# Tiny per-head products moved from VectorE to GpSimd in a two-layer decoder trunk

## The chip, the cores and the metric

One core of one Trainium2 chip runs the whole kernel in one launch. The metric is the device time of that launch in microseconds (us); smaller is better. The engines are named as in the profile: PE is TensorE's matrix multiply, PEld its weight load, DVE is VectorE, ACT is ScalarE, POOL is GpSimd and SP is SyncE, which here issues the loads. Each engine has a queue of its own and works through it in order; a wait at the head of a queue holds everything behind it.

## The reference

The input is x of 256 tokens by 2048 features and a memory of 256 tokens. There are two layers. Layer 0 projects x, sends 1536 columns through a causal pooling mixer and the last 512 through a cross-attention over the memory with 4 heads of 128, projects the joined result, and then runs a squared-ReLU MLP of width 8192. Shared keys and values are then made once. Layer 1 projects x into queries of 12 differential heads (two maps of 64 per head) and 4 memory heads:

```python
def rms_norm(x, g):
    xf = x.astype(jnp.float32)
    y = xf * lax.rsqrt(jnp.mean(xf * xf, axis=-1, keepdims=True) + EPS)
    return (y * g.astype(jnp.float32)).astype(x.dtype)
...
        a = probs(q1b, k1) - lam * probs(q2b, k2)
        return jnp.einsum('bhqk,bkhd->bqhd', a.astype(v.dtype), v)
...
            o = differential_attention(q1, q2, sk1, sk2, sv, lam)
            token_out = (rms_norm(o, subln_norm[b]) * (1.0 - lam_init)).reshape(B, S, DIFF_V_WIDTH)
...
        mem_out = memory_cross_attention(mem_q, mem, mem_norm[i], w_mem_kv[i], mem_q_norm[i], mem_k_norm[i])
        x = x + jnp.concatenate([token_out, mem_out], axis=-1) @ w_out[i]
        x = x + squared_relu_mlp(rms_norm(x, ffn_norm[i]), w_ff1[i], w_ff2[i])
```

EPS is 1e-6. All arithmetic is float32 in the reference.

## The kernel before

**Weights.** All weights lie in memory in the order of use and stream through a ring. For each quad of four 128x128 blocks, ACT makes the rounded high half (`hi_ring`, L157) and DVE the remainder (`lo_ring`, L158: one subtraction of two SBUF tiles). PE multiplies with both halves. The ring has 6 slots, and a quad is prepared up to 3 quads ahead of its use (`Feed.fill`). A quad keeps PE busy for about 1.4 us.

**Attention beside the weights.** The work of the heads is put between the quads. `at(d, fn)` files a function for d quads later, and `tick()` runs what is due after each quad. A differential head (`diff_head`) has four steps. `scores` multiplies queries and keys into PSUM, adds the mask on DVE, takes the row maximum on DVE (`mx`, L1207), multiplies it by the query's scale (L1208), runs four exponentials on ACT (L1211, with their row sums in `z`), and forms `att` from them with reciprocals on DVE. Four quads later `turn` transposes the result on PE (`dt`, L1226). `pv` multiplies by the values and does the per-head RMS norm: two squares with sums on ACT (`o_ss`), `o_v` on DVE, then `rsqrt_cols`, then two scalings into `osb` (L1250). `back` transposes `osb` (`o_t`, L1255) and splits it into `cat`. The third group of four heads lies under the memory queries' projection and is packed closer (`by_pe`: PE adds the mask).

`rsqrt_cols` takes a column of 2 to 16 values per row through ln and exp on ACT (L359, L360), then makes one step of refinement with two products on DVE (L361, L362) and one combined operation (L300).

A memory head has `mem_query` (squares, `stats` two quads later with `rsqrt_cols`) and `mem_head` (scores, maximum `mm_max` at L575 and L576, exponentials, a transposition `mt` at L592, and the product with the values). `mem_head` serves both layers; `mem_query` serves layer 1 alone.

**The order on each queue.** The order in which the program calls instructions is not the order on the engines. A scheduler of the framework places each engine's instructions by when it reckons them ready, and puts semaphore waits between engines.

**Stages in the trace.** Layer 0's heads lie at 84 to 125 us. Layer 1's differential heads and memory heads run from about 1150 to 1276 us, under the projections `q` and `mq` and the start of the output projection `wo`. After that come the residual, the MLP of layer 1, and the end.

Of the kernel before, what the change touches and what calls it, by code (L numbers as in the profile page):

```python
# [13 lines left out]
AF = mybir.ActivationFunctionType  # L14
ALU = mybir.AluOpType
# [3 lines left out]
P = 128  # L19
# [3 lines left out]
EPS = 1e-6  # L23
LAM_INIT = 0.8 - 0.6 * math.exp(-0.3)
# [8 lines left out]
G_PS, G_MQ, G_MK, G_QN, G_KN, G_SUB = 112, 124, 126, 128, 129, 130  # L33
# [229 lines left out]
def program(ctx, tc, plan, dry, xT, memT, par, lam, cst, wst, yT):  # L263
    nc = tc.nc
# [28 lines left out]
    def vt(name):  # L293
        return tp.tile([P, T], F32, tag="v", bufs=6, name=name)
# [4 lines left out]
    def stt(out, a, s, b, op0, op1, **kw):  # L299
        nc.vector.scalar_tensor_tensor(out=out, in0=a, scalar=s, in1=b, op0=op0, op1=op1, **kw)  # L300
# [39 lines left out]
    def gcol(c):  # L340
        return param[:, c : c + 1]
# [10 lines left out]
        stt(t2, mean, EPS, t, ALU.add, ALU.mult)  # L352
        stt(out, t2, 3.0 * CN * CN, h, ALU.subtract, ALU.mult, reverse0=True)

    def rsqrt_cols(out, v):

        n = v.shape[-1]
        w = [tp.tile([P, 16], F32, tag="w8", bufs=8, name="rc")[:, :n] for _ in range(4)]
        nc.scalar.activation(w[0], v, AF.Ln)  # L359
        nc.scalar.activation(w[1], w[0], AF.Exp, bias=lnc, scale=-0.5)  # L360
        nc.vector.tensor_mul(w[2], w[1], w[1])  # L361
        nc.vector.tensor_mul(w[3], w[2], v)  # L362
        stt(out, w[3], 3.0 * CN * CN, w[1], ALU.subtract, ALU.mult, reverse0=True)

    def stat(name):
        return pp.tile([P, T], F32, tag="st", bufs=1, name=name)
# [174 lines left out]
    def mem_query(src, gq, cols):  # L541


        q = vt("mq")
        sq = vt("mq_sq")
        nc.scalar.activation(q, src, AF.Copy, scale=gq)
        nc.scalar.activation(sq, src, AF.Square)
        y = tp.tile([P, 2], F32, tag="m2", bufs=12, name="mq_y")

        def stats():  # L550
            st = stat("st_mq")
            for t in range(2):
                nc.tensor.matmul(
                    st[:, 2 * t : 2 * t + 2], sq[:, t * P : t * P + P], ones_h,
                    start=True, stop=True,
                )
            v2 = tp.tile([P, 2], F32, tag="m2", bufs=12, name="mq_v")
            nc.vector.tensor_mul(v2, st[:, 0:4].rearrange("p (a b) -> p a b", b=2)[:, :, 0], cols[1])
            nc.vector.tensor_scalar_add(v2, v2, EPS)
            rsqrt_cols(y, v2)  # L560
            nc.vector.tensor_mul(y, y, cols[0])

        at(2, stats)
        return q, y

    def mem_head(q, y, k, v, e, pT, out, lag, pv_lag=6):

        def scores():  # L570
            s = pp.tile([P, 2, T], F32, tag="s", bufs=2, name="ms")
            for t in range(2):
                nc.tensor.matmul(s[:, t, :], q[:, t * P : t * P + P], k, start=True, stop=True)
            m = tp.tile([P, 2], F32, tag="m2", bufs=12, name="mm_max")
            nc.vector.tensor_reduce(out=m, in_=s, axis=AX.X, op=ALU.max, negate=True)  # L575
            nc.vector.tensor_mul(m, m, y)  # L576
            z = tp.tile([P, 2], F32, tag="m2", bufs=12, name="mm_sum")
            for t in range(2):
                nc.scalar.activation(
                    e[:, t, :], s[:, t, :], AF.Exp, bias=m[:, t : t + 1], scale=y[:, t : t + 1],  # L580
                    accum_out=z[:, t : t + 1],
                )
            zr = tp.tile([P, 2], F32, tag="m2", bufs=12, name="mm_rec")
            nc.vector.reciprocal(zr, z)
            for t in range(2):
                nc.vector.tensor_scalar_mul(e[:, t, :], e[:, t, :], zr[:, t : t + 1])

        def turn():
            t4 = pp.tile([P, 2, T], F32, tag="t", bufs=1, name="mt")
            for mb in range(2):  # L590
                for t in range(2):
                    nc.tensor.transpose(  # L592
                        t4[:, mb, t * P : t * P + P], e[:, t, mb * P : mb * P + P], ident
                    )
            nc.scalar.copy(pT, t4)

        def pv():
            o = pp.tile([P, T], F32, tag="o", bufs=1, name="mo")
            for mb in range(2):
                nc.tensor.matmul(o, v(mb), pT[:, mb, :], start=mb == 0, stop=mb == 1)  # L600
            nc.scalar.copy(out[:, 0:T], o)
            nc.vector.tensor_sub(out[:, T : 2 * T], o, out[:, 0:T].bitcast(F32))

        at(lag, scores)
        at(lag + 4, turn)
        at(lag + pv_lag, pv)
# [557 lines left out]


    gsub = cp.tile([P, 1], F32, name="gsub")
    nc.vector.tensor_scalar_mul(gsub, gcol(G_SUB), 1.0 - LAM_INIT)
    idb = cp.tile([P, P], BF16, name="idb")
    nc.vector.tensor_copy(idb, ident)
    mkb = cp.tile([P, P], BF16, name="mkb")  # L1170
# [4 lines left out]
    def diff_head(h, q, y, lag, pv_lag, back_lag, by_pe):  # L1175
# [3 lines left out]
        yh = y.rearrange("p (t j m h) -> p t j m h", t=2, j=2, m=2)[:, :, j % 2, :, h % 2]  # L1179
        ez = tp.tile([P, 2], F32, tag="ez", bufs=6, name="ez")  # L1180

        def scores():
            s1 = pp.tile([P, 2, T], F32, tag="s", bufs=2, name="s1")
            s0 = pp.tile([P, 2, P], F32, tag="s", bufs=2, name="s0")
            if by_pe:
                for m in range(2):
                    kk = kT[:, 6 * m + j, :]
                    nc.tensor.matmul(s1[:, m, :], q[:, m, P:T], kk, start=True, stop=False)
                    nc.tensor.matmul(s1[:, m, P:T], idb, mkb, start=False, stop=True)
                for m in range(2):  # L1190
                    kk = kT[:, 6 * m + j, 0:P]
                    nc.tensor.matmul(s0[:, m, :], q[:, m, 0:P], kk, start=True, stop=False)
                    nc.tensor.matmul(s0[:, m, :], idb, mkb, start=False, stop=True)
            else:
                for m in range(2):
                    kk = kT[:, 6 * m + j, :]
                    nc.tensor.matmul(s1[:, m, :], q[:, m, P:T], kk, start=True, stop=True)
                for m in range(2):
                    kk = kT[:, 6 * m + j, 0:P]
                    nc.tensor.matmul(s0[:, m, :], q[:, m, 0:P], kk, start=True, stop=True)  # L1200
                mask = const[:, C_MASK : C_MASK + P].unsqueeze(1).to_broadcast([P, 2, P])
                nc.vector.tensor_add(s1[:, :, P:T], s1[:, :, P:T], mask)
                nc.vector.tensor_add(s0, s0, mask)
            mx = tp.tile([P, 2, 2], F32, tag="m4", bufs=6, name="mx")
            z = tp.tile([P, 2, 2], F32, tag="m4", bufs=6, name="z")
            for t, s in ((1, s1), (0, s0)):
                nc.vector.tensor_reduce(out=mx[:, t, :], in_=s, axis=AX.X, op=ALU.max, negate=True)  # L1207
            nc.vector.tensor_mul(mx, mx, yh)  # L1208
            for t, s, e in ((1, s1, e1), (0, s0, e0)):
                for m in range(2):  # L1210
                    nc.scalar.activation(  # L1211
                        e[:, m, :], s[:, m, :], AF.Exp, bias=mx[:, t, m : m + 1],
                        scale=yh[:, t, m : m + 1], accum_out=z[:, t, m : m + 1],
                    )

            zr = tp.tile([P, 2], F32, tag="m2", bufs=12, name="zr")
            nc.vector.reciprocal(zr, z[:, :, 1])
            stt(zr, zr, nlam, z[:, :, 0], ALU.mult, ALU.mult)
            stt(ez, z[:, :, 0], EPS, z[:, :, 0], ALU.mult, ALU.mult)
            for t, e, dst in ((1, e1, a[:, P : P + T]), (0, e0, a[:, 0:P])):  # L1220
                stt(dst, e[:, 1, :], zr[:, t : t + 1], e[:, 0, :], ALU.mult, ALU.add)

# [6 lines left out]
        def pv():  # L1229
            o = pp.tile([P, 2, P], F32, tag="o", bufs=1, name="do")  # L1230
# [5 lines left out]
            if by_pe:  # L1236
                nc.vector.tensor_copy(osb, o)
                o = osb
            ss = tp.tile([P, 2], F32, tag="m2", bufs=12, name="o_ss")
            junk = vt("o_sq")  # L1240
            for t in range(2):
                nc.scalar.activation(
                    junk[:, t * P : t * P + P], o[:, t, :], AF.Square, accum_out=ss[:, t : t + 1]
                )
            v = tp.tile([P, 2], F32, tag="m2", bufs=12, name="o_v")
            stt(v, ss, 1.0 / P, ez, ALU.mult, ALU.add)
            yo = tp.tile([P, 2], F32, tag="m2", bufs=12, name="o_y")
            rsqrt_cols(yo, v)
            for t in range(2):
                nc.vector.tensor_scalar_mul(osb[:, t, :], o[:, t, :], yo[:, t : t + 1])  # L1250

# [12 lines left out]
    for c in range(3):  # L1264
        ps = pair_of_banks(0, "q1")
        b_tile(ps, "w_in_q", 1, c, x_mx)
        rows, v = query_rows(ps, c1, 64)
        rope(rows, qtab)
        y = query_scale(v, c1)
# [10 lines left out]
    for h in range(4):  # L1280
        ps = mmt("mq1")
        c_tile(ps, "w_in", 1, 12 + h, range(NK), x_mx)
        q, y = mem_query(ps[:, 0:T], mqg1, c1)
# [93 lines left out]
```

## Time and profile before

| | |
|---|---|
| median of 3 runs | 2045.62 us (2045.5 to 2046.13) |
| the profiled execution's own time | 2044.93 us |
| its span, first to last instruction | 2043.1 us |
| PE busy | 2037.2 us |
| DVE busy | 1716.2 us, 3215 instructions |
| ACT busy | 1349.8 us, 2505 instructions |
| POOL busy | 51.9 us, 67 instructions |
| granted TensorE clock | 1.000 of full speed |

The span is the time between the first and the last instruction on the core; the execution's own time is 1.83 us longer. Busy times are sums of the durations of an engine's instructions, without their overlaps. Instructions of one engine can overlap in these records by up to a tenth of a microsecond or so, since the next one starts while the last results of the one before are being written.

### The profile page before, as it was taken

How to read it: one execution, taken by the hardware profiler on the slowest of the kernel's cores; microseconds unless marked ns; L12 is line 12 of the kernel's file. 1: busy time of each engine (PE TensorE's matmuls, PEld its weight loads, DVE VectorE, ACT ScalarE, POOL GpSimd, SP SyncE). 2: the span in 40 equal slices, each digit the busy share in tenths (PEclk: the TensorE clock that was granted, in tenths of full speed). 3: DMA queues.
4: the chain of work that ended last, by engine and by line, in shares of the span. 5: the costliest groups of instructions: out<-in, count | busy, mean ns of one | idle time of the engine just before them, and what ended most of it. 6: DMA issues, size and time to landing. Idle time of an engine off the chain costs nothing.

```text
span 2043.1 us, 32257 instructions
## 1 busy us (share of the span) xinstructions
PE 2037.2 (100%) x11060; PEld 1755.3 (86%) x11060; DVE 1716.2 (84%) x3215; ACT 1349.8 (66%) x2505; POOL 51.9 (3%) x67
## 2 busy tenths in 40 slices
PE   9999999999999999999999999999999999999999
PEld 8888888888888888888888888888888888888888
DVE  8888889889879978999766687889879978988997
ACT  7765566666666756768665697566657666666764
POOL 0001200000000000000000000310000000000000
PEclk9999999999999999999999999999999999999999
DMA  9556556555555555655565543656555555565564
GB/s 314 178 181 190 188 174 206 197 196 197 186 201 202 189 207 191 207 169 182 194 228 186 170 140 103 196 166 207 196 196 205 186 196 196 186 210 195 196 209 135
DMA packets 110470, 390.75 MB, mean 191 GB/s; under 512 B 12256, under 2 KB 14944, under 8 KB 110304
## 3 DMA queue, kind: packets, MB, share of 16 engines
q1 hardware_dynamic: 110160, 388.59, 57.1%
q8 instruction: 86, 1.41, 0.3%
q14 instruction: 80, 0.66, 0.1%
q10 hardware_dynamic: 144, 0.10, 0.0%
HBM read 386.54 MB, written 2.10 MB: 190 GB/s over the span
## 4 chain that ended last, share of the span: by engine, by line
PE 99%; ACT 1%; DVE 1%; issue 0%
PE x_bank L391 33%; PE x_bank L393 16%; PE wo L391 6%; PE p L746 5%; PE p L747 5%; PE p L748 5%; PE wo L393 3%; PE u L391 2%; PE ff L391 2%; PE u L393 1%; PE k L417 1%; PE k L419 1%; PE v L417 1%; PE k L418 1%; PE v L419 1%; PE v L418 1%
## 5 line engine op out<-in xcount | busy, mean ns | idle before, releaser
L157 ACT CAST hi_ring<-raw 128x512 fp32r<-128x512 f32 x1193 | 736.7, 620 | 529.5 <-PE x_bank L391 308.0
L158 DVE TENSOR_TENSOR lo_ring<-raw,hi_ring 128x512 fp32r<-128x512 f32 x1193 | 817.2, 695 | 206.7 <-ACT hi_ring L157 165.5
L391 PE MATMUL x_bank<-fx,hi_ring 128*128 128x512 f32 x1920 | 602.1, 395 | 0.0
L393 PEld LDWEIGHTS x_bank<-fx,lo_ring 128*128 128x128 f32 x1920 | 361.0, 188 | 83.6
L393 PE MATMUL x_bank<-fx,lo_ring 128*128 128x256 f32 x1920 | 377.4, 278 | 0.0
L391 PEld LDWEIGHTS x_bank<-fx,hi_ring 128*128 128x128 f32 x1920 | 301.4, 189 | 9.3
L391 PE MATMUL x_bank<-z,hi_ring 128*128 128x512 f32 x960 | 301.1, 395 | 0.0
L158 DVE TENSOR_TENSOR lo_ring<-slab,hi_ring 128x1024 fp32r<-128x1024 f32 x188 | 230.1, 1224 | 54.3 <-ACT hi_ring L157 53.6
L157 ACT CAST hi_ring<-slab 128x1024 fp32r<-128x1024 f32 x188 | 196.9, 1047 | 73.1 <-PE x_bank L391 36.2
L393 PEld LDWEIGHTS x_bank<-z,lo_ring 128*128 128x128 f32 x960 | 180.5, 188 | 41.7
L393 PE MATMUL x_bank<-z,lo_ring 128*128 128x256 f32 x960 | 188.8, 278 | 0.0
L391 PE MATMUL wo<-cat,hi_ring 128*128 128x512 f32 x512 | 162.5, 398 | 0.5 <-DVE resid L639 0.5
L391 PEld LDWEIGHTS x_bank<-z,hi_ring 128*128 128x128 f32 x960 | 151.9, 189 | 6.5 <-ACT room L672 0.4
L393 PEld LDWEIGHTS wo<-cat,lo_ring 128*128 128x128 f32 x512 | 95.9, 188 | 21.7
L672 ACT COPY room<-x_bank 128x512 f32<-128x512 f32 x180 | 104.9, 583 | 2.0 <-PE x_bank L393 2.0
L393 PE MATMUL wo<-cat,lo_ring 128*128 128x256 f32 x512 | 101.4, 279 | 0.0
L746 PE MATMUL p<-hi_ring,sit 128*128 128x512 f32 x256 | 100.5, 393 | 0.0
L747 PE MATMUL p<-hi_ring,sit 128*128 128x512 f32 x256 | 100.2, 391 | 0.0
L748 PE MATMUL p<-lo_ring,sit 128*128 128x512 f32 x256 | 99.7, 389 | 0.0
L391 PEld LDWEIGHTS wo<-cat,hi_ring 128*128 128x128 f32 x512 | 79.1, 189 | 2.2 <-PE wo L393 0.9
L717 ACT ACTIVATE room<-room 128x256 f32<-128x256 f32 x128 | 53.2, 416 | 39.1 <-DVE room L300 39.1
L746 PE MATMUL p<-hi_ring,z 128*128 128x512 f32 x192 | 75.2, 392 | 0.0
(313 smaller groups left out, 3102.3 us busy)
## 6 DMA issues: line engine op xcount, KB each, us to landing
raw<-in_w SPq DMA_DIRECT2D x595, 512.0 KB, 4.0
slab<-in_w SPq DMA_DIRECT2D x124, 512.0 KB, 3.3
resid<-in_x SPq DMA_DIRECT2D x8, 256.0 KB, 5.9
room<-in_w SPq DMA_DIRECT2D x4, 512.0 KB, 4.2
memraw<-in_mem SPq DMA_DIRECT2D x4, 512.0 KB, 3.6
out_y<-resid SPq DMA_DIRECT2D x16, 128.0 KB, 1.8
memraw<-in_mem SPq DMA_DIRECT2D x7, 256.0 KB, 6.3
raw<-in_w SPq DMA_DIRECT2D x3, 256.0 KB, 3.5
```

What stands on the lines that cost most here:

```text
L157: self.nc.scalar.copy(hi, src)
L158: self.nc.vector.tensor_sub(lo, src, hi.bitcast(F32))
L391: nc.tensor.matmul(ps, hi, xs[:, k, :], start=first and c == 0, stop=False)
L393: nc.tensor.matmul(ps[:, T : 2 * T], lo, xs[:, k, 0:T], start=False, stop=last and c == len(ks) - 1,)
L417: nc.tensor.matmul(ps[t], xl, hi, start=k == 0, stop=False)
L418: nc.tensor.matmul(ps[t], xh, hi, start=False, stop=False)
L419: nc.tensor.matmul(ps[t], xh, lo, start=False, stop=k == NK - 1)
L672: nc.scalar.copy(x, ps)
L717: at(3, lambda: nc.scalar.activation(stage[i % 8], y[:, 0:T], AF.Square))
L746: nc.tensor.matmul(ps, a[1], hi, start=first, stop=False)
L747: nc.tensor.matmul(ps, a[0], hi, start=False, stop=False)
L748: nc.tensor.matmul(ps, a[0], lo, start=False, stop=last)
```

## The change

It concerns operations on two or four columns (128 rows by 2 or 4 values). In `rsqrt_cols`, when called for a differential head's norm or a memory query of layer 1, the two products go to GpSimd. So do the product of the memory query's scale with the row's factor, the products of the maxima with the scales in `mem_head` (both layers) and `diff_head`, the square `ez`, and the sum `o_v`. [...]

```diff
-    def rsqrt_cols(out, v):
+    def rsqrt_cols(out, v, aside=False):
...
+        eng = nc.gpsimd if aside else nc.vector
...
-        nc.vector.tensor_mul(w[2], w[1], w[1])
-        nc.vector.tensor_mul(w[3], w[2], v)
+        eng.tensor_mul(w[2], w[1], w[1])
+        eng.tensor_mul(w[3], w[2], v)
...
-            rsqrt_cols(y, v2)
-            nc.vector.tensor_mul(y, y, cols[0])
+            rsqrt_cols(y, v2, True)
+            nc.gpsimd.tensor_mul(y, y, cols[0])
...
-            nc.vector.tensor_mul(m, m, y)
+            nc.gpsimd.tensor_mul(m, m, y)
...
-    nc.vector.tensor_scalar_mul(gsub, gcol(G_SUB), 1.0 - LAM_INIT)
+    nc.vector.tensor_scalar_mul(gsub, gcol(G_SUB), (1.0 - LAM_INIT) * EPS**-0.5)
...
-            nc.vector.tensor_mul(mx, mx, yh)
+            nc.gpsimd.tensor_mul(mx, mx, yh)
...
-            stt(ez, z[:, :, 0], EPS, z[:, :, 0], ALU.mult, ALU.mult)
+            nc.gpsimd.tensor_mul(ez, z[:, :, 0], z[:, :, 0])
...
                 nc.scalar.activation(
-                    junk[:, t * P : t * P + P], o[:, t, :], AF.Square, accum_out=ss[:, t : t + 1]
+                    junk[:, t * P : t * P + P], o[:, t, :], AF.Square,
+                    scale=(P * EPS) ** -0.5, accum_out=ss[:, t : t + 1],
                 )
...
-            stt(v, ss, 1.0 / P, ez, ALU.mult, ALU.add)
+            nc.gpsimd.tensor_add(v, ss, ez)
...
-            rsqrt_cols(yo, v)
+            rsqrt_cols(yo, v, True)
```

The scheduler places the instructions of the changed kernel anew. In the built order PE's queue differs first where the differential heads' transpositions start, and last early in `wo`; the rest of it is the same instruction for instruction.

## The prediction

> **What bounds the kernel now.** I read the page's busy line first, then the stretches around layer 1's heads, then DVE's groups by shape there, then timelines of single heads.
>
> ```profile
> PE 2037.2 (100%) x11060; PEld 1755.3 (86%) x11060; DVE 1716.2 (84%) x3215; ACT 1349.8 (66%) x2505; POOL 51.9 (3%) x67
> ...
> 1150.00:1170.00 20.00, 19.91 (x104) 16.62 (x103) 14.06 (x38) 14.68 (x39) 0.00 (x0) 1.00 0.43 143
> 1170.00:1190.00 20.00, 19.78 (x106) 16.61 (x105) 18.21 (x67) 17.99 (x53) 0.00 (x0) 1.00 0.37 127
> 1190.00:1210.00 20.00, 20.00 (x121) 17.78 (x120) 16.76 (x56) 16.15 (x53) 0.00 (x0) 1.00 0.52 159
> 1210.00:1230.00 20.00, 19.95 (x156) 18.76 (x155) 18.08 (x64) 17.84 (x55) 0.00 (x0) 1.00 0.42 132
> 1250.00:1270.00 20.00, 19.24 (x116) 16.66 (x116) 16.79 (x60) 14.90 (x52) 0.00 (x0) 1.00 0.31 106
> 1270.00:1290.00 20.00, 19.68 (x113) 16.76 (x112) 17.26 (x33) 11.55 (x25) 5.59 (x7) 1.00 0.56 181
> ```
>
> PE bounds it. A row of the second kind is a stretch of 20 us with the busy time of PE, PEld, DVE, ACT and POOL. DVE reaches 18 of 20 us under the heads, yet PE is idle for only 0.09 + 0.22 + 0.05 + 0.76 + 0.32 = 1.44 us there, and its granted clock is 1.00. Two short restarts after waits add perhaps 1 us that counts as busy. So what a lighter DVE can win is at most about 2.4 us: PE's own work is not changed.
>
> ```profile
> L361 DVE TENSOR_TENSOR rc<-rc 128x2 f32<-128x2 f32 x16 | 2.5, 157 | 1.3 <-ACT rc L360 1.3
> L300 DVE SCALAR_TENSOR_TENSOR ez<-z 128x2 f32<-128x2 f32 x12 | 1.9, 160 | 6.8 <-ACT att L1211 6.7
> L1208 DVE TENSOR_TENSOR mx<-mx,qy 128x4 f32<-128x4 f32 x12 | 1.9, 159 | 0.1
> ```
>
> **What leaves DVE.** Each differential head loses `mx`, `ez`, `o_v` and two `rc`: 12 x 5 = 60. Each memory head of layer 1 loses two `rc` and two products: 16. Layer 0's heads lose one each: 4. That is 80 instructions of about 0.157 us, 12.5 us of DVE's busy time. Less of it is queue time: in a timeline the next independent instruction starts 0.07 to 0.11 us after such a product (1170.44 to 1170.50), so about 7 us. And `ez` stands in a wait anyway (6.7 us idle before it, for ACT), after which the reciprocal waits for ACT again.
>
> **What an operation on POOL costs.** The trace has none on two columns with two inputs. The nearest rows are a memset of 128x2 at 0.10 us and a product of 128x256 at 0.61 us; scaled by columns between them it is about 0.1 us. I take 0.12, since two columns lie next to the memset, and keep 0.10 and 0.61 as ends. From DVE's end to POOL's start the trace has 0.08 to 0.18 us (L639 to L624 and L618), from POOL to POOL 0.09. From POOL to ACT there is no row; DVE to ACT takes 0.04 (1156.97 to 1157.00), and 0.04 to 0.2 is taken. So `mx` costs 0.13 + 0.12 + 0.05 = 0.30 us from the last maximum to the first exponential, where it cost 0.23 (1156.77 to 1157.00): +0.07 per head.
>
> The Trainium skill says in "GPSIMD Engine Reference", section "Engine selection", that elementwise work with two inputs is about twice as slow there; taken as an estimate that makes 0.31 us of 0.157, still under the upper end above.
>
> **The lock.** POOL and DVE do disturb each other:
>
> ```profile
> 200.28 0.61 POOL L624 TENSOR_TENSOR psq<-resid 128x256 f32<-128x256 f32 x1 [3.75 <-DVE resid L639]
> 200.98 1.07 POOL L625 TENSOR_TENSOR acc<-acc,psq 128x256 f32<-128x256 f32 x1
> ...
> 200.59 0.86 DVE L158 TENSOR_TENSOR lo_ring<-raw,hi_ring 128x512 fp32r<-128x512 f32 x1 [0.38 <-ACT hi_ring L157]
> ```
>
> The sum started at 200.98, inside the `lo_ring` subtraction that ended at 201.45, and ended at 202.05: 0.60 us after DVE was done, as long as POOL's product takes alone. It was held until DVE finished. At 183.50 the same: DVE ended at 183.70, POOL at 184.30. The Trainium skill states this in "SBUF — State Buffer", section "Who interferes with whom": a DVE instruction with two SBUF inputs and a GpSimd one that reads SBUF exclude each other, and the later one waits out the whole instruction. The trace agrees (0.60 us above).
>
> Here that means that a product on POOL which comes just after a `lo_ring` (0.69 us) has started costs up to 0.6 us more, and one that comes ahead of it delays DVE by 0.12 at most.
>
> **Who waits.** Head 1 and head 3 show the two places:
>
> ```profile
> 1155.76 1.01 DVE L1207 TENSOR_REDUCE mx<-s 128x2 f32<-128x512 f32 x2
> 1156.81 0.16 DVE L1208 TENSOR_TENSOR mx<-mx,qy 128x4 f32<-128x4 f32 x1
> 1157.24 0.69 DVE L158 TENSOR_TENSOR lo_ring<-raw,hi_ring 128x512 fp32r<-128x512 f32 x1 [0.27 <-issue]
> ...
> 1160.47 0.52 PE L1226 MATMUL dt<-const,att 128*128 128x128 f32 x3
> ```
>
> In the built order a `lo_ring` follows the maxima directly in heads 1, 2, 3 and 5 of the first eight. In head 2 it waits for ACT's cast until after POOL would be done (1164.19 against 1163.95), and in head 5 ACT is busy with other work meanwhile. So two are held in full: 1 and 3. ACT waits at its first exponential, with the next casts behind it; the casts feed slots which PE reads 4 to 10 us later (from the end of each subtraction to PE's first use), so that is covered. If that cover is gone, a late cast stops PE directly. At the turns of the three groups it is thinner: 1.37 us (1183.74), 0.75 (1215.63) and 0.71 (1283.52).
>
> What is not covered is `dt`. From the end of `att` to `dt` the twelve heads have 0.14, 0.87, 0.15, 1.46, 0.92, 0.72, 0.42, 1.50, 4.23, 0.15, 1.00 and 0.56 us, of which about 0.1 is the signal. A delay of 0.07 is lost in these. Heads 1 and 3 with 0.6 lose 0.46 + 0.45 = 0.9 us of PE.
>
> The norm's chain: `o_y` on DVE now waits for ACT's Exp and two products on POOL. In head 3 Exp ends at 1169.89; POOL 0.08 + 0.12 + 0.09 + 0.12 and 0.1 for the signal make 1170.40, where before the second product was through at 1170.59. DVE's next item before `o_y` ends at 1170.08, so DVE stands idle for about 0.3 us, with a mask addition, two scalings and two maxima behind it. That takes back what the five removed instructions gave (5 x 0.08 = 0.4). `o_t` comes 1.3 to 6 us after `osb`, except head 6, where PE waits (1217.04) and the new order has `osb` ahead of a `lo_ring`: 0.2 us won.
>
> Memory heads of layer 1: `mt` follows the scaled `att` by 0.90 and 0.10 us and then waits twice (0.76 us is the longest PE stall here). Its chain now changes engine five times, at +0.1 us each, but skips DVE's queue, which took 3.1 us from Exp (1256.99) to the exponentials (1260.10). I put this at zero, with 1 us either way. Layer 0's four `mx` have 2.2 us (`mt` at 90.69, `att` at 88.51): nothing. The scaled square and `gsub` cost nothing: same instructions with other constants.
>
> **Sum.** Lost 0.9; won 0.4 (0.2 at head 6's `o_t`, 0.2 of the 0.68 us that PE idles outside the memory heads' stall); memory heads 0: +0.5 us. On the profiled execution 2044.93 becomes 2045.4; the median stands 0.69 above it, so 2045.62 becomes about 2046.1. That is no change: 0.2%, 4.1 us, is about what a measurement of this kernel can tell from none.
>
> **Rivals.**
> - *The lock holds nearly every product* (slower). If each head's chain comes late by 0.6 us, the `dt` slacks give 0.46 + 0.45 + 0.18 + 0.45 + 0.04 = 1.6 us and the memory heads (0.90, 0.10, none, none) 1.7: 2048.9. At 1.0 us late they give 4.1 and 3.0: 2052.7. It decides from 0.7 us per head (2.1 + 2.0). For it: the hold of a full `lo_ring` is 0.69 us, and there are up to four products in a chain. Against it: DVE has such subtractions for about half of the time, and cat, mask and maximum read PSUM. This is the rule named above, taken at its worst.
> - *DVE's relief wins* (faster). All 1.44 us of idle PE and the restarts go: 2043.2 to 2044.2, which is still within 0.2%. Faster than that needs a gain that no row shows.
> - *The reordering decides.* ACT puts four exponentials (2.0 us) ahead of a cast in the third group, and PE's queue is shuffled until `wo`. With 0.7 to 1.4 us of cover at three turns, 1 us late costs 0.3 each, 2 us late up to 1.3 each: 2046.5 to 2049.5, mostly within 0.2%.
>
> **Chances.** Forecast 0.50, relief within 0.2% 0.13, reordering within 0.2% 0.12: together 0.75 the same. Lock and reordering beyond 4.1 us: 0.21 slower. Faster by more: 0.04. The likeliest gives 2046.1. The range goes from 2043.5 (nearly all idle PE won) to 2051.0 (chains late by 0.9 us), leaving out some 0.15.
>
> **What would show it.** POOL has 80 more instructions, mostly 0.1 to 0.2 us, some near 0.7 beside a `lo_ring`. DVE's busy time falls by some 12 us, and new DVE waits for POOL stand at `o_y`, 0.2 to 0.4 us each. PE's idle time between 1145 and 1290 us stays within 1 to 3 us. The forecast is wrong if products on POOL take over 0.6 us on their own, if PE waits for `lo_ring`, or if `dt` and `mt` wait in most heads.

## The result

The kernel with the change takes 2048.7 us (median of 22 runs, 2048.26 to 2050.12), the kernel before it 2045.32 us on the same chip (22 runs, 2045.0 to 2046.48). The ratio of the two is 1.0017, with a 95% interval of 1.0011 to 1.0023. So the change costs 3.4 us. That is inside the 0.2% that was set as "no change", and inside the predicted range. But it is a loss that the interval tells from nothing, and it is 2.6 us above the forecast of 2046.1 us.

The profiled execution of the changed kernel took 2048.7 us with a span of 2046.9 us, 3.8 us more than before. Some 0.5 us of these are there at 50 us already, long before anything that the change touches, and still at 1150 us: that is the start-up's own spread (one of the runs below, e5_split, has 1.6 there). The rest arises between 1150 and 1290 us.

The first line is the page's busy line, the others the same stretches of 20 us that the prediction showed (PE, PEld, DVE, ACT, POOL, granted clock, DMA share, GB/s), now of the changed kernel.

```profile
PE 2039.0 (100%) x11060; PEld 1753.9 (86%) x11060; DVE 1708.0 (83%) x3135; ACT 1349.3 (66%) x2505; POOL 73.6 (4%) x147
...
1150.00:1170.00 20.00, 19.92 (x102) 16.43 (x101) 13.51 (x33) 14.57 (x37) 0.91 (x5) 1.00 0.46 148
1170.00:1190.00 20.00, 19.27 (x106) 16.20 (x105) 17.06 (x52) 17.23 (x53) 2.43 (x11) 1.00 0.41 129
1190.00:1210.00 20.00, 19.75 (x111) 17.15 (x110) 14.63 (x41) 15.63 (x51) 3.31 (x14) 1.00 0.42 141
1210.00:1230.00 20.00, 19.67 (x150) 18.06 (x150) 16.17 (x51) 18.66 (x58) 2.62 (x11) 1.00 0.39 127
1230.00:1250.00 20.00, 19.25 (x148) 17.63 (x146) 13.90 (x41) 15.41 (x54) 4.66 (x18) 1.00 0.32 106
1250.00:1270.00 20.00, 18.97 (x121) 16.20 (x121) 14.54 (x44) 15.23 (x52) 5.26 (x18) 1.00 0.26 80
1270.00:1290.00 20.00, 20.00 (x115) 17.13 (x114) 15.99 (x30) 11.83 (x24) 4.96 (x6) 1.00 0.52 177
```

Eighty instructions left DVE and POOL has eighty more, as built. DVE is lighter in every one of these stretches, and PE is idle in six of the seven, for 0.08 + 0.73 + 0.25 + 0.33 + 0.75 + 1.03 = 3.17 us in place of 1.44. The granted clock stays at 1.00. One of these stretches of the kernel before the prediction does not show; PE was never idle in it:

```profile
1230.00:1250.00 20.00, 20.00 (x157) 18.80 (x157) 15.34 (x56) 16.20 (x56) 0.00 (x0) 1.00 0.25 80
```

The growth of the idle time, 1.7 us, is only about half of the loss. PE's busy time grew too, by 1.8 us for the same 11060 matmuls (2037.2 to 2039.0). The prediction had put such time down to restarts after waits; the runs do not say where it lies.

The new groups on POOL, by shape (us busy in total, mean ns of one, then the idle time before them):

```profile
L1249 POOL TENSOR_TENSOR o_v<-o_ss,ez 128x2 f32<-128x2 f32 x12 | 3.9, 322 | 33.4 <-ACT o_sq L1244 33.4
L1210 POOL TENSOR_TENSOR mx<-mx,qy 128x4 f32<-128x4 f32 x12 | 3.7, 306 | 919.1 <-DVE mx L1209 914.1 <-DVE rc L364 5.0
L1221 POOL TENSOR_TENSOR ez<-z 128x2 f32<-128x2 f32 x12 | 2.3, 195 | 19.6 <-ACT att L1213 19.6
L578 POOL TENSOR_TENSOR mm_max<-mm_max,qy 128x2 f32<-128x2 f32 x4 | 2.2, 544 | 107.7 <-DVE mm_max L577 107.7
L578 POOL TENSOR_TENSOR mm_max<-mm_max,mq_y 128x2 f32<-128x2 f32 x4 | 1.7, 430 | 1.9 <-DVE mm_max L577 1.9
```

A product of two or four columns takes 0.20 us on POOL (`ez`, at 195 ns), where DVE took 0.16. The groups with a larger mean contain single instructions of 0.34 to 1.05 us. There are 14 of these among the 80, and they sum to 8.5 us. With the other 66, at about 0.20, they make 21.5 us, and POOL's busy time has grown by 21.7.

Head 3 shows one of the 14. First POOL, then DVE, then PE, from the timelines:

```profile
1173.24 0.58 POOL L1210 TENSOR_TENSOR mx<-mx,qy 128x4 f32<-128x4 f32 x1 [2.05 <-DVE mx L1209]
1172.16 1.01 DVE L1209 TENSOR_REDUCE mx<-s 128x2 f32<-128x512 f32 x2
1173.09 0.68 DVE L158 TENSOR_TENSOR lo_ring<-raw,hi_ring 128x512 fp32r<-128x512 f32 x1
1177.32 0.52 PE L1228 MATMUL dt<-const,att 128*128 128x128 f32 x3 [0.47 <-DVE att L300]
```

The maxima end at 1173.17. Before POOL has its signal, DVE starts the next `lo_ring` subtraction, which ends at 1173.77, and the product on POOL ends at 1173.82, 0.05 us later. Twelve of the 14 are in layer 1, and all twelve end 0.05 to 0.10 us after a DVE subtraction of two SBUF tiles: eleven after a `lo_ring`, one after `room`. Three and a half microseconds on, PE waits 0.47 us at `dt`.

The norm's chain of head 1, which stands on DVE just ahead of head 3's maxima, POOL and then DVE:

```profile
1170.72 0.20 POOL L363 TENSOR_TENSOR rc<-rc 128x2 f32<-128x2 f32 x1 [0.64 <-ACT rc L362]
1171.00 0.20 POOL L364 TENSOR_TENSOR rc<-rc,o_v 128x2 f32<-128x2 f32 x1
1171.23 0.16 DVE L300 SCALAR_TENSOR_TENSOR o_y<-rc 128x2 f32<-128x2 f32 x1 [0.48 <-POOL rc L364]
```

DVE stands idle for 0.48 us, with a mask addition, two scalings and the two maxima behind `o_y`. That is how head 3's maxima come to end next to a ready `lo_ring`: counted from the first `tq` they end 1.0 us later than before (22.95 us against 21.93), and 0.9 us later already with the norm's part alone (e3_norm below). The step behind them did not get longer. From the last maximum to the first exponential head 3 took 1.06 us before, when the product stood behind other work in DVE's queue, and 0.69 with the change, its hold included.

Two answers of the view of waits, first of DVE and ACT, then of PE, between 1145 and 1310 us (what waited, for what; us in total, times, longest):

```profile
DVE o_y L300 <- POOL rc L364: 7.7, 11, 1.3
ACT att L1213 <- POOL mx L1210: 3.7, 7, 1.1
```

```profile
PE dt L1228 <- DVE att L300: 0.7, 2, 0.5
PE o_t L1258 <- DVE mq_v L560: 0.6, 1, 0.6
PE ms L575 <- ACT att L1213: 0.5, 1, 0.5
PE dt L1228 <- ACT att L1165: 0.2, 1, 0.2
...
```

Three more waits of 0.2 us follow, at `tq`, `s` and `do`. None of these stands in the same view of the kernel before, and the two that did (0.76 us at `mt` and 0.33 at `wo`) are gone.

The second of the two waits at `dt` (0.25 us, 1203.38, head 6) has no held `mx` behind it: that head's product took 0.20 us, but its maxima ended 2.0 us later than before, counted from the first `tq`. Ahead of them DVE waited 0.86 us at an `o_y` (1197.66) whose `o_v` had taken 0.64 us, held by a `lo_ring` (1195.88).

### The profile page after: what moved, and what is told of

Same layout as the page of the kernel before. It is cut to its first block, busy times and chain, and to the rows that moved or that the text cites. A ratio compares the mean times of both kernels' runs of the same rounds, so it can differ in the third digit from the quotient of the medians.

```text
span 2046.9 us, 32284 instructions
## 1 busy us (share of the span) xinstructions
PE 2039.0 (100%) x11060; PEld 1753.9 (86%) x11060; DVE 1708.0 (83%) x3135; ACT 1349.3 (66%) x2505; POOL 73.6 (4%) x147
## 4 chain that ended last, share of the span: by engine, by line
PE 96%; ACT 2%; DVE 1%; issue 0%; POOL 0%; POOLq 0%; DVEq 0%
PE x_bank L393 33%; PE x_bank L395 16%; PE wo L393 6%; PE p L748 5%; PE p L749 5%; PE p L750 5%; PE wo L395 3%; PE u L393 2%; PE ff L393 2%; PE u L395 1%; PE k L419 1%; PE k L421 1%; PE v L419 1%; PE k L420 1%; PE v L421 1%; PE v L420 1%
```

## The experiments

All edits are against the kernel before or against the changed kernel, as said. Medians and ratios go by the kernel before on the same chip. An interval of these ratios is about 0.0009 to either side, 1.8 us, so most single parts can't be told from nothing by the clock alone. Beside it stands a finer measure from each kernel's one trace: the **stretch**, PE's time from the first `tq` transposition until 320 of the 512 products of `wo` with high halves are through (256 of them are layer 0's). It holds the same work in every kernel and leaves out the start-up's spread. I split it at the first matmul of `mq`: the *first part* holds the first two groups of differential heads, the *second part* the third group and the memory heads.

| run | median us (before) | ratio, 95% interval | stretch us | first part | second part |
|---|---|---|---|---|---|
| before | | | 133.28 | 56.68 | 76.60 |
| the change | 2048.70 (2045.32) | 1.0017, 1.0011 to 1.0023 | 136.33 | 57.82 | 78.51 |
| e1_ez | 2045.39 (2045.47) | 0.9999, 0.9990 to 1.0008 | 133.24 | 56.68 | 76.56 |
| e2_mx | 2046.25 (2045.47) | 1.0004, 0.9995 to 1.0012 | 133.80 | 56.86 | 76.94 |
| e3_norm | 2046.12 (2045.47) | 1.0003, 0.9994 to 1.0011 | 133.87 | 57.03 | 76.84 |
| e4_mem | 2045.83 (2045.47) | 1.0001, 0.9993 to 1.0010 | 133.54 | 56.70 | 76.84 |
| f1_nomem | 2046.68 (2045.30) | 1.0005, 0.9996 to 1.0015 | 134.27 | 57.80 | 76.47 |
| f2_nomx | 2047.45 (2045.30) | 1.0009, 1.0000 to 1.0019 | 134.94 | 57.05 | 77.89 |
| f3_split | 2048.31 (2045.30) | 1.0015, 1.0006 to 1.0024 | 135.83 | 57.15 | 78.68 |
| f4_nonorm | 2047.17 (2045.30) | 1.0009, 0.9999 to 1.0018 | 134.83 | 56.86 | 77.97 |
| g1_mmdve | 2045.08 (2045.52) | 0.9998, 0.9989 to 1.0007 | 133.23 | 57.85 | 75.38 |
| g2_mmonly | 2046.55 (2045.52) | 1.0005, 0.9996 to 1.0015 | 134.49 | 57.75 | 76.74 |
| e6_splitd | 2044.24 (2045.52) | 0.9993, 0.9984 to 1.0002 | 131.53 | 56.62 | 74.91 |
| e5_split | 2044.45 (2045.52) | 0.9995, 0.9986 to 1.0004 | 131.66 | 56.37 | 75.29 |

How fine the stretch is shows where two kernels have the same work in the same order: e1_ez repeats both parts of before to 0.04 us, and e4_mem, which changes nothing ahead of the memory heads, repeats the first part to 0.02. PE's order in the first part is also one and the same in the changed kernel, f1_nomem, g1_mmdve and g2_mmonly, whose first parts lie within 0.1 us of each other, in e2_mx and f4_nonorm (no difference), and in e3_norm and f2_nomx (0.02). The stretch's growth of the changed kernel, 3.05 us, is nearly all of the 3.4 us of the median; through the runs the two shifts agree within 0.6 us.

### Each part alone: e1_ez, e2_mx, e3_norm, e4_mem

**e1_ez**: the kernel before with the square on POOL, and epsilon as a factor; the rest stays on DVE. ACT's square is scaled by (128 EPS)^-1/2, so that `ez` is a plain square and `o_v` a plain sum, and `gsub` takes the factor EPS^-1/2 (both not shown here).

```diff
+            nc.gpsimd.tensor_mul(ez, z[:, :, 0], z[:, :, 0])
-            stt(ez, z[:, :, 0], EPS, z[:, :, 0], ALU.mult, ALU.mult)
...
+            nc.vector.tensor_add(v, ss, ez)
-            stt(v, ss, 1.0 / P, ez, ALU.mult, ALU.add)
```

> Only the 12 squares ez go to GpSimd, with epsilon taken out as a factor; all other products stay on VectorE. PE's queue has the same order as before. By 'stretch' is meant PE's time from the first query transposition (tq) to the 320th of the 512 wo matmuls with the high half: 133.28 us before, 136.34 us with the whole change. Theory A (the loss is made of waits on GpSimd in chains that PE waits for): ez is needed two quads later and is in nobody's way, so the stretch is 0 to 0.5 us shorter, and the time the same or 0.5 us less. Rival B (the new order of PE's queue makes the loss): the order is the same, so 0 too. Rival C (each product on GpSimd disturbs VectorE through the shared port, wherever it stands): 12 of 80 products, 0.3 to 0.5 us longer.

Measured: no difference, in the time (0.9999) or in the stretch (-0.04). PE's queue is in the order of before, matmul for matmul. So the constants cost nothing, and twelve products on POOL which PE does not wait for cost nothing. Rival C, 0.3 to 0.5 us for these twelve wherever they stand, is out.

**e2_mx**: the kernel before with `nc.gpsimd.tensor_mul(mx, mx, yh)`, nothing else.

> Only the 12 products of the maxima with the scales (mx) go to GpSimd. Theory A: the exponentials start later by 0.1 us where VectorE is free, and by up to 0.6 us where a lo_ring subtraction has started just before; with 0.15 us between att and dt in three heads, the stretch is 0.5 to 1.5 us longer, and PE's waits stand at dt. Rival B (order): PE's queue is reordered about as much as with the whole change, so most of its loss, 2 to 3 us, and the waits stand elsewhere than at dt. Rival C (port, anywhere): 0.3 to 0.5 us.

Measured: 0.52 us, 0.18 of it in the first part: theory A's size, at its lower end, but not its place. PE's largest new wait stands not at `dt` but at a `tq`, 0.83 us in the third group. ACT's wait for the products:

```profile
ACT att L1211 <- POOL mx L1208: 2.3, 6, 0.6
```

Three of the twelve products are held by a `lo_ring`, all in the second part. They take 1.0 us more than three free ones, and the second part grew by 0.34: most of the hold is covered when the product alone is moved.

**e3_norm**: the kernel before with epsilon as a factor, `o_v` and the two products of the norm's `rsqrt_cols` on POOL.

```diff
-            rsqrt_cols(yo, v)
+            rsqrt_cols(yo, v, True)
...
+            nc.gpsimd.tensor_add(v, ss, ez)
```

> Only the differential heads' norm goes to GpSimd: o_v and the two products rc, 36 operations, with epsilon as a factor; ez is a plain product on VectorE. Theory A: o_y stands on VectorE for 0.3 to 0.5 us in most heads (7.7 us in all with the whole change), with masks and maxima of the next scores behind it; the stretch is 0.5 to 1.5 us longer. Rival B (order): a third less reordering than with mx alone, up to 1.5 us, without new waits of VectorE for GpSimd showing before them. Rival C (port, anywhere): 0.9 to 1.5 us, with o_y hardly waiting.

Measured: 0.59 us, 0.35 of it in the first part. The wait at `o_y` is the largest new one, three quarters of that with the whole change:

```profile
DVE o_y L300 <- POOL rc L363: 5.7, 11, 1.2
```

That is theory A. But 5.7 us of DVE's waiting cost PE only 0.6: most of it lies in DVE's own slack.

**e4_mem**: the kernel before with the memory heads' part alone (`rsqrt_cols(y, v2, True)`, and `mq_y` and `mm_max` on POOL).

> Only the memory heads go to GpSimd: in layer 1 the two rc, the product mq_y and the product mm_max of each of four heads, in layer 0 the four mm_max. Theory A: four products of 0.2 us and five changes of engine in one chain make mt later by 0.5 us in each head of layer 1, of which three have less than 0.2 us of cover; stretch 1 to 2 us longer, all of it after 1220 us; layer 0 nothing. Rival B (order): some 2 us, before and after the memory heads alike. Rival C (port, anywhere): 0.4 us.

Measured: 0.26 us, all of it in the second part, where theory A wanted 1 to 2 us and the order rival 2. ACT waits for `mm_max` at all four exponentials of layer 1:

```profile
ACT att L580 <- POOL mm_max L577: 4.0, 4, 2.0
```

The four parts alone add up to -0.04 + 0.52 + 0.59 + 0.26 = 1.33 us. Together they cost 3.05. More than half of the loss belongs to no part: it comes from parts acting on each other, in the orders that the scheduler makes of them, and the next runs ask which.

### One part taken back: f1_nomem, f2_nomx, f4_nonorm

**f1_nomem**: the whole change, but the memory heads (both layers) on DVE as before. **f2_nomx**: the whole change, but the differential heads' `mx` on DVE. **f4_nonorm**: the whole change, but `o_v` and the norm's two products on DVE.

> The whole change without the memory heads: all 60 products and sums of the differential heads on GpSimd, the memory heads of both layers on VectorE. One part alone made PE's stretch (133.28 us before, 136.33 with the whole change) longer by 0.52 (mx), 0.59 (norm), 0.26 (memory heads) and -0.04 (ez), 1.33 in sum, and each of the three won about 1 us back in its last part, between the 256th and the 320th wo matmul. Theory A (losses add, but the idle time of PE at the end, there without the change too, is won back only once): 1.4 us longer, of which up to the first mq matmul 1.1, in the next 64 of them 0.6, and 0.8 won back at the end. Rival D (norm and mx together are worse than their sum, since the wait at o_y pushes the maxima behind it into lo_ring): 2 us or more, the excess before the first mq matmul. Rival B (order): no less than 2.5 us, since the order of PE's queue stays that of the whole change in the differential heads.

> The whole change with the 12 mx products back on VectorE. Theory A: up to the first mq matmul 0.4 us longer (as with the norm alone), 0.6 in the next 64, 1.9 up to the 256th wo matmul, 0.8 won back: 2.0 us. Rival D: before the first mq matmul no more than the norm's own 0.35, and the whole about 1.5 us. Rival B (order): 2.5 us or more.

> The whole change with the differential heads' norm (o_v and rc) back on VectorE. Theory A: up to the first mq matmul 0.2 us longer (as with mx alone), 0.8 in the next 64, 1.8 up to the 256th wo matmul, 0.8 won back: 2.0 us. Rival D: the excess before the first mq matmul, 0.6 us with the whole change, goes with the norm too, and the whole is about 1.5 us. Rival B (order): 2.5 us or more.

Measured, in the first part: f1_nomem 1.12 us, the same as the whole change (1.14); f2_nomx 0.37, as e3_norm alone (0.35); f4_nonorm 0.18, as e2_mx alone (0.18). So the first part is settled: 0.2 us by `mx`, 0.35 by the norm, and 0.6 more only where both are moved. In the second part: f1_nomem costs nothing (-0.13), while f2_nomx costs 1.29 and f4_nonorm 1.37. With the memory heads moved as well, either of the other parts is enough for more than a microsecond. The whole stretch grew by 0.99, 1.66 and 1.55 us. So the order rival (2.5 or more) is out in each; theory A (1.4, 2.0, 2.0) was too high each time. Rival D had its 1.5 about right for the last two, and too much for f1_nomem (2 or more), though the excess in the first part is there as it said.

### What the 0.6 us are: f3_split

The whole change, but the product of the maxima cut in two, each half directly behind its own maximum, so that the first runs while DVE reduces from PSUM:

```diff
             for t, s in ((1, s1), (0, s0)):
                 nc.vector.tensor_reduce(out=mx[:, t, :], in_=s, axis=AX.X, op=ALU.max, negate=True)
-            nc.gpsimd.tensor_mul(mx, mx, yh)
+                nc.gpsimd.tensor_mul(mx[:, t, :], mx[:, t, :], yh[:, t, :])
```

> The whole change, but each mx product is cut in two, one behind each of the two maxima. The first half then runs on GpSimd while VectorE takes the second maximum from PSUM, so that no lo_ring can hold it; the second half can be held, but ACT needs it only for its third exponential, some 1.1 us later. Theory A (the shared port holds mx): ACT no longer waits for GpSimd at the first exponential (3.7 us with the whole change, below 0.5 here), the first part of the stretch is shorter by 0.5 us than with the whole change, and the whole by 0.5 to 1 us. Rival (the hold on mx costs PE nothing, since the maxima are late anyway): ACT's wait goes, the stretch stays within 0.2 us of 136.33. Rival B (order): any value, but not tied to ACT's waits.

Measured: the first part falls from 57.82 to 57.15. That is 0.67 us, and both waits for `att` at `dt` are gone. So the two parts meet in the stretch from the last maximum to the first exponential, though PE's order is a new one here too, and the run does not separate the two. What was expected of ACT's wait failed: it was to fall under 0.5 us and fell from 3.7 to 2.8.

```profile
ACT att L1212 <- POOL mx L1209: 2.8, 5, 0.9
```

Three half products of `mx` are still held; in head 3 it is the second half, and the first exponential starts as the second maximum ends. And the second part does not improve (78.68 after 78.51): the median stays at 1.0015.

### Which half of the memory heads: g1_mmdve, g2_mmonly

**g1_mmdve** is the whole change with one instruction of each memory head taken back to DVE, **g2_mmonly** the whole change with the memory heads' `rsqrt_cols` and `mq_y` taken back.

```diff
-            nc.gpsimd.tensor_mul(m, m, y)
+            nc.vector.tensor_mul(m, m, y)
```

```diff
-            rsqrt_cols(y, v2, True)
-            nc.gpsimd.tensor_mul(y, y, cols[0])
+            rsqrt_cols(y, v2)
+            nc.vector.tensor_mul(y, y, cols[0])
```

> The whole change, but the products of the memory heads' maxima (mm_max, both layers) stay on DVE; their rsqrt products and mq_y are on POOL. The stretch, PE's time from the first tq transposition to the 320th matmul of wo's high halves, was 133.28 us before, 136.33 with the whole change and 134.27 with the whole change but all of the memory heads on DVE, so the memory heads' share is 2.06 us. Theory 1 (the held product of the maxima carries it: in three of the four heads it took 0.51 us, and ACT waited up to 2.0 us for it): stretch 134.2 to 134.8. Theory 2 (the chain of rsqrt products and mq_y carries it, by leaving DVE's queue in another order): 135.8 to 136.4. Theory 3 (neither; a head that comes late by either ends in the same stall): each part alone brings about half, 135.0 to 135.6.

> The whole change, but the memory heads' rsqrt products and mq_y stay on DVE; only mm_max is on POOL there. Theory 1 (the held product of the maxima): stretch 135.6 to 136.4. Theory 2 (the rsqrt chain): 134.2 to 134.8. Theory 3 (half each): 135.0 to 135.6.

Measured: g1_mmdve 133.23, so the single product takes back 3.1 us, and the kernel is as fast as before with 72 instructions on POOL. g2_mmonly 134.49. No theory had both. Against f1_nomem, which has neither, the chain alone gains 1.04 us and the product alone costs 0.22: the 2.06 us take the chain *and* the product on POOL. The stretches of g1_mmdve that answer to the fifth and sixth of the changed kernel:

```profile
1230.00:1250.00 20.00, 20.00 (x158) 18.87 (x158) 14.84 (x45) 16.03 (x57) 3.41 (x16) 1.00 0.33 106
1250.00:1270.00 20.00, 19.80 (x129) 17.61 (x128) 16.17 (x48) 16.53 (x56) 3.54 (x16) 1.00 0.32 105
```

PE idles 0.20 us where the changed kernel has 1.78. But the held product is not the direct reason. From the start of the maximum to the first exponential the first three memory heads take 1.37, 1.06 and 1.37 us in the changed kernel, and 1.49, 1.38 and 1.43 in g1_mmdve, where DVE has other work ahead of the product: the step itself is not longer on POOL. What differs is the order that the scheduler gives to PE and ACT, and what meets a held product in it. In the changed kernel PE comes to the second `ms` soon after a `dt`, and waits 0.46 us for ACT's exponentials; in g1_mmdve part of the `do` matmuls are ahead of it, and it does not wait. The exponentials themselves are late in both. In the changed kernel their product `mx` stands in POOL's queue behind a norm's `rc`, which waited for ACT and was then held: it starts at 1240.13, 0.61 us after the maxima's end (1239.52). In g1_mmdve it stands behind a held `rc` too, and is as late. The largest stall of the changed kernel can be followed to a held product (POOL, DVE, PE):

```profile
1263.98 1.05 POOL L1249 TENSOR_TENSOR o_v<-o_ss,ez 128x2 f32<-128x2 f32 x1 [2.12 <-ACT o_sq L1244]
1263.09 1.28 DVE L158 TENSOR_TENSOR lo_ring<-raw,hi_ring 128x512 fp32r<-128x512 f32 x2
1264.29 0.68 DVE L182 TENSOR_TENSOR room<-slab,slab 128x512 f32<-128x512 f32 x1
1266.18 0.16 DVE L300 SCALAR_TENSOR_TENSOR o_y<-rc 128x2 f32<-128x2 f32 x1 [1.20 <-POOL rc L364]
1266.56 0.41 PE L1258 MATMUL o_t<-const,osb 128*128 128x128 f32 x2 [0.64 <-DVE mq_v L560]
```

The sum `o_v` starts in the second of two `lo_ring`, DVE goes on without a pause into another subtraction of two SBUF tiles, and POOL is let go only after that one (1264.97), 0.85 us late. Then DVE waits 1.20 us at `o_y`, and PE 0.64 at `o_t`, the matmul that needs the scaled `osb`. (The view names `mq_v`, a DVE instruction which ended just then; `osb` follows it behind the same `o_y`.) In g1_mmdve the same `o_v` takes 0.22 us and PE waits 0.20.

### Two versions against the kernel before: e6_splitd, e5_split

Both put only `ez` on POOL and cut the product of the maxima in two; **e6_splitd** has the halves on DVE, **e5_split** on POOL.

```diff
                 nc.vector.tensor_reduce(out=mx[:, t, :], in_=s, axis=AX.X, op=ALU.max, negate=True)
-            nc.vector.tensor_mul(mx, mx, yh)
+                nc.vector.tensor_mul(mx[:, t, :], mx[:, t, :], yh[:, t, :])
```

> A candidate to beat the kernel before: ez on POOL with epsilon as a factor, the product of the maxima cut in two on DVE, each directly behind its own maximum, so that the first exponential need not wait for the second maximum (0.5 us earlier); all else on DVE as before. If the time from the last maximum to the first exponential is what dt waits for, the stretch is 132.8 to 133.2 against 133.28 before, and the median 0.1 to 0.5 us under the kernel before. If twelve more DVE instructions and a new order cost what the earlier exponential wins, 133.2 to 133.7. In both cases too small for the median to tell.

> As the one before, but the two half products of the maxima are on POOL. Theory of the lock: the first half runs beside the second maximum, which reads PSUM, and is not held; the second is still held where a lo_ring follows, and with it the third exponential only, which has two exponentials ahead of it (about 1 us): stretch 133.0 to 133.5. Theory that a hop to POOL costs by itself in every head (0.08 us and 0.20 for the product): 133.4 to 133.9, about the 133.80 of the undivided product on POOL.

Measured: 131.53 and 131.66, better than either expectation; the medians are 1.3 and 1.1 us under before, with intervals that just reach 1. In the first part the reason given does not show: in e6_splitd's first head both halves come behind the second maximum, and the part gains 0.06 us (0.31 in e5_split). The gain is in the second part. PE has no wait of 0.15 us or more left there in e6_splitd, and one of 0.34 at `tq` in e5_split; the 0.76 us at `mt` and the 0.33 at `wo` are gone in both.

```profile
1250.00:1270.00 20.00, 20.00 (x126) 16.98 (x125) 16.62 (x60) 15.56 (x50) 0.00 (x0) 1.00 0.33 106
1270.00:1290.00 20.00, 20.00 (x116) 17.38 (x115) 17.58 (x30) 11.06 (x21) 6.35 (x8) 1.00 0.61 208
```

In that part the split does what it was meant to do. In heads 10 to 12 the first exponential starts 2.6, 0.9 and 1.5 us before the second maximum has ended, and the `att` of these heads is ready 2.7, 5.0 and 4.5 us earlier than before, counted from the first `tq`. Head 12, from the timelines:

```profile
1242.60 0.16 DVE L1208 TENSOR_TENSOR mx<-mx,qy 128x2 f32<-128x2 f32 x1
1244.06 0.56 ACT L1211 ACTIVATE att<-s,mx,qy 128x256 f32<-128x256 f32 x1
1245.13 0.42 DVE L1207 TENSOR_REDUCE mx<-s 128x2 f32<-128x256 f32 x1
```

That is not enough by itself: f3_split has these heads as early, and its second part is the longest of all. The runs show that the stalls are gone; how much of it is the split and how much the new order of the queues stays open.

## Why the prediction was right, and where it was not

**The outcome** it held likeliest, a change too small for 0.2%, came, and the time is inside the range. That owes something to luck: the range was 7.5 us wide, and 2048.7 us fits the rival of the reordering (2046.5 to 2049.5) and not the forecast's 2046.1. Nor is 0.2% what a measurement can tell here: 22 runs of each kernel tell 0.06%, and the loss is three times that. The forecast's sum of +0.5 us was 2.6 to 2.9 us short, and the mis-sized terms can be named.

**Memory heads, put at 0 with 1 us either way.** This is the term that failed. Beside the rest of the change they cost 2.06 us (136.33 less f1_nomem's 134.27), and alone 0.26 us. The prediction weighed each edit by itself against the trace of before; no single edit was worth 1 us, but together they were. The two stalls of before at the end of the section (0.76 and 0.33) also served as a reserve. e3_norm shows it: from the 256th to the 320th product of `wo`, with the same matmuls in between as before, it takes 30.64 us against 31.42, and PE idles 0.22 us there against 1.09. A part that comes late alone can eat these stalls first; in the whole change other stalls stand there (0.95 us). For the other runs it is not shown as cleanly, since matmuls cross these borders.

**`dt`, put at 0.9 us.** Nearly the right size (the first part lost 1.14), by partly the wrong road. The hold by a `lo_ring` is as described: it lasts to the end of DVE's instruction and 0.05 us more. But head 1, which was to be held, was not: POOL's product started at 1157.40, ahead of the `lo_ring`, and ended at 1157.60. In head 3 the hold came, but on top of maxima that ended 1.0 us later; the forecast added it to a step of 0.23 us, as in head 1, where head 3 had 1.06 before and 0.69 after. The third such loss, head 6's 0.25 us, had no held `mx` at all. What the prediction missed is that the wait at `o_y` moves the maxima, and with them who meets a `lo_ring`: f1_nomem lost 0.6 us more than e2_mx and e3_norm together. The prediction reckoned that wait and the lock in separate terms. Nor did it ask what stands ahead of `mx` in POOL's own queue: in heads 5 and 11 the product starts 1.1 and 0.6 us after the maxima, behind a norm's `rc`.

**The operation on POOL, taken as 0.12 us**, measured 0.20 undisturbed; the ends 0.10 and 0.61 held it. The estimate by the Trainium skill, "GPSIMD Engine Reference", section "Engine selection" (about twice as slow, 0.31 us), was too high by about as much as mine was too low: at these sizes the ratio is 0.20 to 0.16. The way from maximum to exponential came out at 0.32 us in head 1, predicted 0.30: 0.08 and 0.04 us of signals in place of 0.13 and 0.05 made up for the slower product.

**The wait at `o_y`, put at 0.3 us of idle DVE per head**, was 0.48 in the chain that the prediction looked at (it calls it head 3's; it is head 1's norm, ahead of head 3's maxima) and 0.7 on the mean of the eleven that waited, for the same reason: two products at 0.20 behind ACT's exponential, and now and then a hold. The 0.4 us per head that DVE's removed instructions were to give back did not cover it. DVE's busy time fell by 8.2 us and not by 12; the 80 durations do sum to 12.6, but the page counts overlaps once, so 8.2 is close to the 7 us of queue time in the prediction.

**The 0.4 us won** (at head 6's `o_t` and in PE's idle time) did not show anywhere: PE's idle time grew from 1.44 to 3.17 us. That is just above the 1 to 3 us which was named as what would be seen. The range's upper end does not come out of the prediction's own slacks either: heads late by 0.9 us give 3.3 + 2.6 us, 2051.5 and not 2051.0.

**The rivals.** *The lock holds nearly every product* did not happen: 14 of 80 were held, three of the twelve `mx`. The rule behind it, in the Trainium skill's "SBUF — State Buffer", section "Who interferes with whom", agrees with the trace in the twelve of layer 1. Where two DVE instructions of the kind stand back to back there, POOL was kept out through both once (1263.98 above), and let in between them three times (at 1204.50, 1231.66 and 1258.26 the product ended with the second `lo_ring` under way). *DVE's relief* did not happen: DVE got lighter by 8 us and waits longer. *The reordering* gave 2046.5 to 2049.5 us, and the time lies there; small edits move the second part between 74.9 us (e6_splitd) and 78.7 (f3_split), and the price of an operation, 0.20 us for 0.16, does not make such steps. How much of them is order was not separated. But the places it named, casts behind four exponentials and slots read late, are not those where PE waits.

**What stays open.** The first part's 1.14 us are accounted for by runs, though each of these has an order of PE's queue that goes with it. Of the second part's 1.91 us, the runs show that they need the memory heads' chain and `mm_max` on POOL together, beside another part. One stall of 0.64 us is followed to a held product, one of 0.46 to a product that queued on POOL and to the order of `ms`; the rest is small waits and restarts, which differ in every version. How much is the hold and how much the order would take a run with the changed kernel's order and the products on DVE; it was not tried, since the scheduler makes the order anew for each version.

## What to carry to other kernels

Moving tiny operations to an idle engine shortens the busy engine's sum, but adds a signal each way and a foreign schedule to a chain; look at who is queued behind the instruction that now waits. Price parts of a change together where they lie on one chain: here the parts alone summed to 1.3 us and cost 3.1 together, in part because slack was there only once. Look at the idle engine's own queue too: a product that was ready stood behind one that waited. And where a scheduler places the instructions, try a version or two that hardly differ: g1_mmdve differs from the changed kernel in one tiny product per memory head, and the stretch in 3.1 us, as much as the change cost.

## What the hardware showed beyond that

- A two-input operation on 128x2 or 128x4 values takes 0.195 to 0.20 us on POOL and 0.157 on DVE; On POOL a next one that needs the result starts 0.28 us after the one before (1170.72, 1171.00), an independent one 0.14 (1190.34, 1190.48), and on DVE an independent one some 0.1 us after.
- The 14 held products of two or four columns ended 0.05 to 0.10 us after a DVE instruction on two SBUF inputs. In layer 1, 26 that began inside a DVE instruction of another kind (a maximum, a mask, `cat`, `osb`), most of which read PSUM, took 0.20 us. Where two instructions on SBUF inputs follow each other without a gap, POOL was let in between them in some cases (0.34 us at 1204.15, between two `lo_ring`) and not in others (1.05 us at 1263.98, through `lo_ring` and `room`). What decides that the runs do not show.
- The other way round, nothing was seen of the small products: three `lo_ring` that began inside one of 0.20 us (1157.50, 1218.53 and 1243.93) took 0.68 to 0.69 us like the rest, and the 1193 `lo_ring` of 128x512 from `raw` sum to 828.8 us before and 828.0 with the change. A wide product does delay DVE: in the kernel before, a `lo_ring` that began at 1290.59, inside POOL's `psq` (128x256, 1290.40 to 1291.01), took 0.97 us.
